# Left-side halves that land in the slots they are split into, sums built in place, and plain blocks run in pairs

## The chip, the core and the metric

The kernel runs on one core of one Trainium2 chip. The metric is the device time of one launch in microseconds (us). The kernel before took 2222.46, 2223.57 and 2224.67 us in three runs, a median of 2223.57 us. Engines are named as in the profile: PE is TensorE, DVE is VectorE, ACT is ScalarE, POOL is GpSimd, and SP is SyncE, which only issues DMAs here.

## The reference

A two-layer trunk on two request batches of 256 and 512 rows with the same weights, so 768 rows of width 2048. All data is float32.

```python
def _even_layer(x, ...):                       # layer 0
    z = _rmsnorm(x, g) @ w_in                  # q, k, v, f, ga, gf
    a = _window_attention(q, k, v, rel_bias, sink) * silu(ga)
    fo = _fourier(f, w_f, b_f) * silu(gf)
    return x + concatenate([a, fo]) @ w_out

def _odd_layer(x, ...):                        # layer 1
    z = _rmsnorm(x, g) @ w_in                  # h, bg, cg, gc, u, v, gd
    co = (bg * _short_conv(cg * h, conv_w)) * silu(gc)
    so = _spatial_gate(u, v, v_gain, w_s, b_s) * silu(gd)
    return x + concatenate([co, so]) @ w_out
```

`_rmsnorm` scales each row by the inverse root of its mean square and by a gain per column.

## The kernel before

Everything is held transposed: 128 features by 768 rows are one k-tile, and 16 k-tiles k are the left side of a product. A k-tile has two halves s of 384 rows. Each float32 product is made of three matmuls of a high and a low part (`three`: xh·wh, xl·wh, xh·wl), so every left half and every weight tile is split: ACT casts the high part (L131), and DVE subtracts it from the float32 value and writes the low part (L132; L245 and L246 where a gain is multiplied in).

Four stages follow each other: the even input projection with attention and Fourier mixing (to 801.8 us in the profile), the even output projection "stage 1" (`Out(1, ...)`), the odd input projection "stage 2" (the V columns first, 576 matmuls of 512 columns, then 24 Strassen products with the gates), and the odd output projection "stage 3" (`Out(3, ...)`). An output projection has 16 blocks of 128 output features. Blocks 0 to 3 are plain: 96 matmuls of 384 columns each. The other 12 go in 6 pairs, each by one Strassen step (`strassen`): 7 products of 8 k-tiles by 3 parts, 168 matmuls of 384 columns a pair, where two plain blocks take 192. The left quarters are A11, A12 (half 0, k-tiles 0 to 7 and 8 to 15) and A21, A22 (half 1). The products also need three sums of left quarters, S1 to S3, and S4 in place of A21; each is split into high and low.

Three times the whole left side is exchanged. At B (801.8 us) the concatenated layer-0 branches, kept in DRAM as `cat`, become the left side of stage 1. At C (1078.7 us) x1, the residual, becomes that of stage 2, and at D (1941.8 us) `cat` of layer 1 becomes that of stage 3. An exchange at B or D loads 16 k-tiles (`load_cat`, L332, at B through `row` tiles of 768 columns; at D through `ev` and `big` tiles, L902 to L905), and `build_sums` (L351) loads every k-tile again as pairs of 768-column tiles `big0` and `big1` (one of each), makes S1, S3, S2 and S4 of them (L358 to L364) in `ev` tiles, splits the sums, and writes S4 to DRAM. While the last plain block runs (`last_use`, L380), `fill` (L368) loads S4 over A21. At C the halves are loaded through `ev` tiles (L756 to L762).

PE runs its matmuls in program order. The order of ACT, DVE, POOL and SP is set by a scheduler when the kernel is built, and each engine runs its list strictly in order: what stands behind a waiting instruction waits too. SP is one list for all DMAs. There are 5 `ev` tiles of 128x384 and 5 weight tiles `wr` of 128x1024 (512 KB). The eight accumulators of PE (`bank`) hold 128x512 each; a plain block takes two, one for each half, and DVE adds the residual to a finished bank (L399), which frees it for another block. Strassen's results leave through L461 and its neighbours.

Of the kernel before, what the change touches and what calls it, by code (L numbers as in the profile page):

```python
# [17 lines left out]
P = 128  # L18
# [3 lines left out]
T = TP + TS  # L22
# [13 lines left out]
QLATE = (2, 0, 1, 3)  # L36
PW = T + 4
KV = ((8, 9, 10, 11, 12, 13, 14, 15, 0, 1, 2, 3, 4, 5, 6, 7), range(16))
# [54 lines left out]
def trunk(ctx, tc, x_t, w_in_e, w_fn, w_out_e, w_in_o, w_sv, w_out_o, w_f, w_st, b_s, sink, rel_bias,  # L93
# [143 lines left out]

    def x_slots(k, s):
        hi = xn.tile([P, H], F32R, name=f"xh{k}_{s}", tag=f"xh{k}_{s}")
        lo = xn.tile([P, H], F32R, name=f"xl{k}_{s}", tag=f"xl{k}_{s}")  # L240
        xs[k][s] = (hi, lo)
# [37 lines left out]
    class Stream:  # L279
# [13 lines left out]
        def block(self, b, tag="z", qs=range(4), flip=False, done=None):  # L293
            for q in qs:
                weights.ahead(weights.at[self.n, b, q] + RING)
                for s in ((1, 0) if flip else (0, 1)):
                    for k in range(4 * q, 4 * q + 4):
                        self.step(b, k, s, tag if tag == "z" else tag[s], k == 4 * qs[0], k == 4 * qs[-1] + 3)
                        if done:
                            done(k, s)  # L300
            return self.take(b)
# [30 lines left out]
    def load_cat():  # L332
        for k in range(KT):
            t = kept.pop(k, None)
            if t is None:
                t = row_tile()
                for s in range(2):
                    nc.sync.dma_start(out=t[:, SL[s]], in_=cat[k][:, SL[s]])
            for s in range(2):
                x_slots(k, s)  # L340
                split(*xs[k][s], t[:, SL[s]])

    late = []

    def ev():
        return late[0].tile([P, H], F32, name="ev", bufs=5)
# [4 lines left out]
    def build_sums(load, sums, order, every):  # L351

        for j in order:
            a, b = (big(i)[:, :T] for i in range(2))
            load(j, a)
            load(j + KH, b)
            s1, s3 = ev(), ev()
            nc.vector.tensor_add(out=s1, in0=a[:, SL[1]], in1=b[:, SL[1]])  # L358
            split(*sums[1][j], s1)
            nc.vector.tensor_sub(out=s3, in0=a[:, SL[0]], in1=a[:, SL[1]])  # L360
            split(*sums[3][j], s3)
            nc.vector.tensor_sub(out=s1, in0=s1, in1=a[:, SL[0]])  # L362
            split(*sums[2][j], s1)
            nc.vector.tensor_sub(out=s3, in0=b[:, SL[0]], in1=s1)  # L364
            nc.sync.dma_start(out=s4d[j], in_=s3)
            yield every

    def fill(k, h, src, t):  # L368
        nc.sync.dma_start(out=t, in_=src)
        x_slots(k, h)  # L370
        split(*xs[k][h], t)

    class Out:
# [3 lines left out]
        def __init__(self, n, pairs, qs, res, result):  # L377
            self.n, self.pairs, self.qs, self.res, self.result = n, pairs, qs, res, result

        def last_use(self, k, s):  # L380
            if s == 1 and k < KH:
                fill(k, 1, s4d[k], ev())

        def run(self):
            st = Stream(self.n)

            def load(k, t):
                nc.sync.dma_start(out=t, in_=cat[k])

            pipe.spawn(build_sums(load, sums, BUILD, BUILD_AT))  # L390
            for b in PLAIN:
                last = b == PLAIN[-1]
                if last:
                    pipe.flush()
                z = st.block(b, qs=self.qs if b == PLAIN[0] else range(4), flip=last, done=self.last_use if last else None)
                for h in range(2):
# [595 lines left out]
```

## Time and profile before

| | us |
|---|---|
| median of three runs | 2223.57 |
| the profiled execution, by the device's clock | 2220.93 |
| its span in the profile | 2219.2 |
| PE busy | 2130.9 (96%) |
| DVE busy | 1430.6 (64%) |
| ACT busy | 906.0 (41%) |
| bytes moved by DMA | 251.99 MB, mean 114 GB/s |

The span is cut below into stretches, each of which lies between two ends of a stage. A group of rows in the next section but one has a line for each stretch: the busy time of every engine in it with the number of its instructions, the TensorE clock that was granted as a share of full speed, the busy share of the DMA engines, and what they moved. A stretch in which PE is busy from end to end is bound by PE, and a stretch in which it is not is where another engine or a transfer decides. The rows of a timeline give start, duration and count of merged instructions, and in brackets the idle time just before with what ended it.

### The profile page before, as it was taken

To read this page: it belongs to the slowest core of one execution; us is meant where nothing else is said; L and a number is where in the kernel's file an instruction comes from. 1 tells how busy PE (TensorE), PEld (TensorE's weight loads), DVE (VectorE), ACT (ScalarE), POOL (GpSimd) and SP (SyncE) were. 2 spreads that over 40 slices of the span, in tenths; PEclk is the share of its full clock that TensorE was granted. 3 is DMA by queue.
4 is the path that set the end of the run, shared out by engine and by line. 5 is a ranking of instruction groups with operands and counts; after the bars stand their busy time and mean duration, and the time that the engine had idled before them with its cause. 6 is when DMAs were issued, how large, how long until landed. Compare 5 with 4: busy or idle time off the path is not lost.

```text
span 2219.2 us, 31587 instructions
## 1 busy us (share of the span) xinstructions
PE 2130.9 (96%) x12034; PEld 2082.8 (94%) x12034; DVE 1430.6 (64%) x2450; ACT 906.0 (41%) x1761; POOL 74.3 (3%) x75
## 2 busy tenths in 40 slices
PE   7999999999999986999799999999999999978999
PEld 6999999999999986999688999999999999968999
DVE  8435746737737655666676666666667777766665
ACT  6323444434534542433534333333334555533332
POOL 5000000000000000222000000000000000000000
PEclk9999999999999997999899999999999999989999
DMA  6512122121121155444568222222222322465442
GB/s 225 131 69 85 49 72 74 48 84 63 59 79 58 39 196 174 147 134 133 178 231 295 98 77 74 81 83 84 83 84 93 100 91 100 146 215 173 131 133 72
DMA packets 108737, 251.99 MB, mean 114 GB/s; under 512 B 11773, under 2 KB 56233, under 8 KB 108585
## 3 DMA queue, kind: packets, MB, share of 16 engines
q1 hardware_dynamic: 108584, 249.98, 34.2%
q8 instruction: 94, 1.54, 0.3%
q14 instruction: 59, 0.48, 0.1%
HBM read 210.58 MB, written 42.49 MB: 114 GB/s over the span
## 4 chain that ended last, share of the span: by engine, by line
PE 88%; DMA 5%; DVE 4%; ACT 2%; issue 1%; SPq 0%; DVEq 0%; ACTq 0%
PE bank L117 87%; DMA big<-cat 3%; PE bank L127 1%; DMA xr<-in_x_t_dram 1%; DVE xl L246 1%; DMA ev<-cat 1%; DMA ev<-x 0%; ACT xh L245 0%; DVE wl L132 0%; DVE xl L132 0%; DVE s1l L132 0%; ACT sc L681 0%; DVE ev L362 0%; DVE ev L358 0%; DVE s3l L132 0%
## 5 line engine op out<-in xcount | busy, mean ns | idle before, releaser
L117 PE MATMUL bank<-xh,wh 128*128 128x384 f32 x2560 | 865.5, 338 | 49.0 <-DVE ev L399 43.4
L117 PE MATMUL bank<-xl,wh 128*128 128x384 f32 x2560 | 862.6, 337 | 2.9 <-DVE xl L132 2.5
L117 PE MATMUL bank<-xh,wl 128*128 128x384 f32 x2560 | 861.3, 336 | 0.0
L131 ACT CAST wh<-wr 128x512 fp32r<-128x512 f32 x728 | 450.4, 621 | 915.6 <-PE bank L117 748.2
L132 DVE TENSOR_TENSOR wl<-wr,wh 128x512 fp32r<-128x512 f32 x728 | 503.9, 695 | 350.1 <-ACT wh L131 341.6
L117 PEld LDWEIGHTS bank<-xh,wh 128*128 128x128 f32 x2560 | 484.5, 189 | 52.5 <-DVE ev L399 44.7
L117 PEld LDWEIGHTS bank<-xl,wh 128*128 128x128 f32 x2560 | 484.8, 189 | 5.8 <-DVE xl L132 5.5
L117 PEld LDWEIGHTS bank<-xh,wl 128*128 128x128 f32 x2560 | 484.3, 189 | 0.0
L117 PE MATMUL bank<-wh,xh 128*128 128x512 f32 x288 | 116.5, 404 | 18.7 <-ACT xh L245 18.7
L117 PE MATMUL bank<-wl,xh 128*128 128x512 f32 x288 | 115.0, 399 | 0.6 <-DVE wl L132 0.6
L117 PE MATMUL bank<-wh,xl 128*128 128x512 f32 x288 | 114.8, 399 | 0.0
L117 PE MATMUL bank<-s2h,wh 128*128 128x384 f32 x288 | 97.1, 337 | 0.0
L117 PE MATMUL bank<-s1h,wh 128*128 128x384 f32 x288 | 97.0, 337 | 0.0
L117 PE MATMUL bank<-s1h,wl 128*128 128x384 f32 x288 | 96.9, 336 | 0.0
L117 PE MATMUL bank<-s3h,wl 128*128 128x384 f32 x288 | 96.8, 336 | 0.0
L117 PE MATMUL bank<-s2l,wh 128*128 128x384 f32 x288 | 96.8, 336 | 0.0
L117 PE MATMUL bank<-s2h,wl 128*128 128x384 f32 x288 | 96.8, 336 | 0.0
L117 PE MATMUL bank<-s3h,wh 128*128 128x384 f32 x288 | 96.7, 336 | 0.0
L117 PE MATMUL bank<-s1l,wh 128*128 128x384 f32 x288 | 96.6, 336 | 0.0
L117 PE MATMUL bank<-s3l,wh 128*128 128x384 f32 x288 | 96.6, 336 | 0.0
L117 PEld LDWEIGHTS bank<-wh,xh 128*128 128x128 f32 x288 | 56.0, 195 | 31.1 <-ACT xh L245 19.5
L640 DVE RECIPROCAL nrt<-nrt 128x384 f32<-128x384 f32 x32 | 81.5, 2548 | 4.8 <-ACT nrt L639 4.8
(197 smaller groups left out, 2483.1 us busy)
## 6 DMA issues: line engine op xcount, KB each, us to landing
wr<-in_w_in_o_dram SPq DMA_DIRECT2D x96, 512.0 KB, 3.3
wr<-in_w_in_e_dram SPq DMA_DIRECT2D x72, 512.0 KB, 3.3
wr<-in_w_out_e_dram SPq DMA_DIRECT2D x32, 512.0 KB, 3.4
wr<-in_w_out_o_dram SPq DMA_DIRECT2D x32, 512.0 KB, 4.0
big<-cat SPq DMA_DIRECT2D x32, 384.0 KB, 3.9
big<-x SPq DMA_DIRECT2D x28, 384.0 KB, 3.8
wr<-in_w_sv_dram SPq DMA_DIRECT2D x16, 512.0 KB, 4.0
ev<-x SPq DMA_DIRECT2D x40, 192.0 KB, 3.3
```

The costliest lines, as they stand in the source:

```text
L117: nc.tensor.matmul(out, lhsT=lhs, rhs=rhs, start=start, stop=stop, skip_group_check=go_on)
L127: nc.tensor.transpose(out=out, in_=in_, identity=ident)
L131: nc.scalar.copy(out=hi, in_=src)
L132: nc.vector.tensor_sub(out=lo, in0=src, in1=hi.bitcast(F32))
L246: nc.vector.scalar_tensor_tensor(out=lo, in0=src, scalar=g, in1=hi.bitcast(F32), op0=ALU.mult, op1=ALU.subtract)
L640: nc.vector.reciprocal(out=rt, in_=rt)
```

## The change

The left side lives in 113 slots of 128x384. Seven roles (A11, A12, A21, A22, S1, S2, S3) of eight k-tiles each have a pair of slots, one for the high and one for the low part, and one slot is spare. A half is loaded into the low slot of its pair as float32. Its high part goes to the pair's high slot, its low part to the spare slot, and the slot that held the float32 value is the new spare (`fill`). Which slots play which role is changed at every exchange (`move`): the new roles are dealt to the old slots in the order in which the last Strassen step of the stage before reads them last (`FREED`). `build_sums` loads four halves into slots of S1, S2 and S3, computes the sums in place and splits them by way of the spare slot. `big0`, `big1` are no longer its landing tiles. There are 4 `ev` tiles in place of 5, and while Strassen steps run, the spare slot serves as a further one (`extra`). The plain blocks run as two pairs: `duo` walks through the k-tiles once for two blocks and both halves, with four accumulators, and the second pair uses the other four. The order of loads at C and D is changed.

```diff
+FREED = ("A11", "S1", "S2", "A12", "S3", "A22", "A21")
...
     def out_order(src, layer, pairs):
-        first = range(4) if layer == 1 else QLATE
-        return [(src, layer, b, q) for b in PLAIN for q in (first if b == PLAIN[0] else range(4))] + [(src, layer, b, q) for b in pairs for q in range(14)]
+        plain = [(src, layer, b, q) for i in range(0, len(PLAIN), 2) for q in range(4) for b in PLAIN[i:i + 2]]
+        return plain + [(src, layer, b, q) for b in pairs for q in range(14)]
...
+    def move(*roles):
+
+        old = [[where[r, j] for j in range(KH)] for r in FREED]
+        for r, o in zip(roles, old):
+            for j in range(KH):
+                where[r, j] = o[j]
...
+        def duo(self, bs, tags, done):
+
+            for q in range(4):
+                weights.ahead(weights.at[self.n, bs[0], q] + RING)
+                for k in range(4 * q, 4 * q + 4):
+                    for s in range(2):
+                        for b, t in zip(bs, (tags[:2], tags[2:])):
+                            self.step(b, k, s, t[s], k == 0, k == KT - 1)
                         if done:
                             done(k, s)
...
     def ev():
-        return late[0].tile([P, H], F32, name="ev", bufs=5)
+        return late[0].tile([P, H], F32, name="ev", bufs=4)
+
+    def extra(dtype=F32):
+
+        return slot(spare[0], dtype) if lent[0] else ev()
...
         for j in order:
-            a, b = (big(i)[:, :T] for i in range(2))
-            load(j, a)
-            load(j + KH, b)
-            s1, s3 = ev(), ev()
-            nc.vector.tensor_add(out=s1, in0=a[:, SL[1]], in1=b[:, SL[1]])
-            split(*sums[1][j], s1)
-            nc.vector.tensor_sub(out=s3, in0=a[:, SL[0]], in1=a[:, SL[1]])
-            split(*sums[3][j], s3)
-            nc.vector.tensor_sub(out=s1, in0=s1, in1=a[:, SL[0]])
-            split(*sums[2][j], s1)
-            nc.vector.tensor_sub(out=s3, in0=b[:, SL[0]], in1=s1)
-            nc.sync.dma_start(out=s4d[j], in_=s3)
+            ids = [i for r in ("S1", "S2", "S3") for i in where[r, j]]
+            a0, a1, b1, b0 = (slot(i, F32) for i in ids[:4])
+            for k, h, t in ((j, 0, a0), (j, 1, a1), (j + KH, 1, b1), (j + KH, 0, b0)):
+                load(k, h, t)
+            if every > 5:
+                yield 3.0
+            nc.vector.tensor_add(out=b1, in0=a1, in1=b1)
+            nc.vector.tensor_sub(out=a1, in0=a0, in1=a1)
+            nc.vector.tensor_sub(out=a0, in0=b1, in1=a0)
+            nc.vector.tensor_sub(out=b0, in0=b0, in1=a0)
+            nc.sync.dma_start(out=s4d[j], in_=b0)
+            for i, src, at in ((2, a0, (ids[4], ids[5])), (3, a1, (ids[0], spare.pop())), (1, b1, (ids[1], ids[3]))):
+                where[f"S{i}", j] = list(at)
+                sums[i][j] = slots((f"S{i}", j))
+                split(*sums[i][j], src)
+            spare.append(ids[2])
             yield every
 
-    def fill(k, h, src, t):
+    def fill(k, h, src, g=None):
+        at = where[quarter(k, h)]
+        t = slot(at[1], F32)
         nc.sync.dma_start(out=t, in_=src)
+        at[1], spare[0] = spare[0], at[1]
         x_slots(k, h)
-        split(*xs[k][h], t)
+        if g is None:
+            split(*xs[k][h], t)
+        else:
+            split_gain(k, h, t, g)
...
         if b == PLAIN[0]:
             nc.scalar.activation(out=rr[:, SL[h]], in_=o, func=AF.Square)
         else:
-            sq = ev()
+            sq = extra()
             nc.scalar.activation(out=sq, in_=o, func=AF.Square)
             nc.gpsimd.tensor_add(out=rr[:, SL[h]], in0=rr[:, SL[h]], in1=sq)
...
-    Out(1, PAIRS_E, range(4), x_t, keep_sum).run()
+    Out(1, PAIRS_E, (4, 5, 6, 7), (0, 1, 2, 3), x_t, keep_sum).run()
...
-    Out(3, PAIRS_O, QLATE, x1, finish).run()
+    Out(3, PAIRS_O, (0, 1, 2, 3), (4, 5, 6, 7), x1, finish).run()
```

Three places show how the engines' lists are changed. A row is the line, the operation and its tiles, then the width, and in brackets the engines and DMA queues whose results it waits for.

First SP at B, before, around the DMAs that write the last k-tiles of `cat` (`cat9` to `cat11`) and the weights `wr`:

```order
155 L184 DMA wr_7851<-in_w_out_e_dram 128x1024 [waits DMAHW4_49,DVE_49]
156 L310 DMA cat10_7533<-at_6647 128x768 [waits DVE_49]
157 L184 DMA wr_7936<-in_w_out_e_dram 128x1024 [waits DMAHW5_49,DVE_49]
158 L338 DMA row_7538<-cat0_3081 128x384
159 L338 DMA row_7538<-cat0_3081 128x384 [waits DMAHW6_49]
160 L338 DMA row_7549<-cat1_3084 128x384 [waits DMAHW7_49,PE_49]
```

The same place of the change:

```order
153 L184 DMA wr_7497<-in_w_out_e_dram 128x1024 [waits DMAHW3_49,DVE_49]
154 L341 DMA cat9_7532<-at_6647 128x768 [waits DVE_49]
155 L409 DMA slot1_7542<-cat0_3081 128x384 [waits PE_49]
156 L409 DMA slot3_7558<-cat1_3084 128x384 [waits PE_49]
157 L409 DMA slot5_7574<-cat2_3087 128x384 [waits DMAHW4_49,PE_49]
158 L409 DMA slot7_7590<-cat3_4564 128x384 [waits DMAHW5_49,PE_49]
159 L409 DMA slot33_7550<-cat0_3081 128x384 [waits DMAHW6_49,PE_49]
```

The loads of the new left side now stand right behind `cat9`, and each waits only for PE's last read of the slot, while before they stood behind `cat10` and two weight tiles.

Second DVE at B, before, where the first plain block's results (L399) stand between the sums (L358 to L364 and the splits s1l, s2l, s3l):

```order
927 L358 TENSOR_TENSOR ev_7879<-big0_7875,big1_7876 128x384 [waits DMAHW2_49,DMAHW0_49]
928 L360 TENSOR_TENSOR ev_7880<-big0_7875 128x384
929 L132 TENSOR_TENSOR s1l6_7722<-ev_7879,s1h6_7721 128x384 [waits Activation_49]
930 L132 TENSOR_TENSOR s3l6_7754<-ev_7880,s3h6_7753 128x384 [waits Activation_49]
931 L362 TENSOR_TENSOR ev_7879<-ev_7879,big0_7875 128x384 [waits DVE_49]
932 L364 TENSOR_TENSOR ev_7880<-big1_7876,ev_7879 128x384 [waits DVE_49]
933 L399 TENSOR_TENSOR ev_7926<-bank_7780,ev_7926 128x384 [waits DMAHW6_49,DMAHW3_49]
```

The change, where the first pair's results are L446, the sums L394 to L397, and `wl_8233` is a weight tile of the second pair (blocks 2 and 3, k-tiles 4 to 7):

```order
957 L446 TENSOR_TENSOR ev_8156<-bank_7805,ev_8156 128x384 [waits PE_49]
958 L446 TENSOR_TENSOR ev_8161<-bank_7813,ev_8161 128x384 [waits DMAHW5_49,PE_49]
959 L132 TENSOR_TENSOR slot80_8122<-slot67_8105,slot66_8121 128x384 [waits Activation_49]
960 L446 TENSOR_TENSOR ev_8166<-bank_7809,ev_8166 128x384 [waits DMAHW6_49]
961 L396 TENSOR_TENSOR slot68_8180<-slot84_8182,slot68_8180 128x384 [waits DVE_49]
962 L394 TENSOR_TENSOR slot86_8207<-slot71_8206,slot86_8207 128x384 [waits DMAHW7_49,DMAHW6_49]
963 L397 TENSOR_TENSOR slot85_8183<-slot85_8183,slot68_8180 128x384 [waits DMAHW3_49,DVE_49]
964 L132 TENSOR_TENSOR slot83_8126<-slot82_8106,slot67_8125 128x384 [waits DMAHW3_49,Activation_49]
965 L132 TENSOR_TENSOR slot101_8194<-slot68_8180,slot100_8193 128x384 [waits Activation_49]
966 L395 TENSOR_TENSOR slot71_8206<-slot70_8205,slot71_8206 128x384 [waits DMAHW5_49,DVE_49]
967 L132 TENSOR_TENSOR wl_8233<-wr_7886,wh_8232 128x512
```

The results still stand between the sums, and the weight tile of the second pair stands behind 56 rows of sums, splits and results, from row 911 on.

Third DVE at C in the change, around the last result of stage 1 (L510) and the first low parts of x1 (L268, the line that was L246):

```order
1158 L510 TENSOR_TENSOR ev_10021<-bank_9954,ev_10021 128x384 [waits PE_49]
1159 L132 TENSOR_TENSOR wl_10408<-wr_10106,wh_10407 128x512 [waits Activation_49]
1160 L268 SCALAR_TENSOR_TENSOR slot15_10204<-slot112_10201,sm_83,slot0_10203 128x384 [waits DMAHW2_49,Pool_49]
1161 L268 SCALAR_TENSOR_TENSOR slot112_10210<-slot33_10207,sm_83,slot2_10209 128x384 [waits DVE_49]
1162 L132 TENSOR_TENSOR big0_10393<-rr_85,big0_10393 128x384 [waits DMAHW4_49,Activation_49]
1163 L268 SCALAR_TENSOR_TENSOR slot33_10216<-slot35_10213,sm_83,slot4_10215 128x384 [waits DMAHW5_49,DVE_49]
...
1168 L268 SCALAR_TENSOR_TENSOR slot43_10246<-slot45_10243,sm_83,slot14_10245 128x384 [waits DMAHW2_49,DVE_49]
1169 L268 SCALAR_TENSOR_TENSOR slot45_10252<-slot81_10249,sm_83,slot65_10251 128x384 [waits DMAHW3_49,DVE_49]
```

The low parts stand in one chain in which each takes the slot that the one before it has freed, and the first goes to slot 15, which POOL still reads as the square of the last result. Row 1169 is the low part of k-tile 8 in half 1.

## Rows read from the trace of the kernel before

**Rows 1.** The page: busy time of each engine, and the chain by engine

```profile
PE 2130.9 (96%) x12034; PEld 2082.8 (94%) x12034; DVE 1430.6 (64%) x2450; ACT 906.0 (41%) x1761; POOL 74.3 (3%) x75
...
PE 88%; DMA 5%; DVE 4%; ACT 2%; issue 1%; SPq 0%; DVEq 0%; ACTq 0%
```

**Rows 2.** Waits of PE: line waited for, us in total, times, longest us

```profile
PE bank L117 <- DVE ev L399: 43.4, 4, 18.1
PE bank L117 <- ACT xh L245: 18.7, 3, 9.1
```

**Rows 3.** Busy time by stretch (count), granted clock, DMA share, GB/s

```profile
802.00:870.00 68.00, 41.78 (x204) 38.99 (x204) 42.80 (x84) 28.26 (x58) 0.00 (x0) 0.81 0.59 196
...
1078.50:1100.00 21.50, 8.24 (x20) 6.03 (x20) 12.34 (x23) 12.56 (x23) 0.99 (x1) 0.68 0.74 225
1100.00:1220.00 120.00, 120.00 (x538) 99.65 (x537) 89.09 (x145) 54.53 (x103) 0.16 (x3) 1.00 0.76 258
...
1942.00:2007.00 65.00, 41.73 (x205) 38.90 (x206) 39.74 (x77) 23.62 (x48) 0.00 (x0) 0.80 0.66 212
```

**Rows 4.** The chain in order of time at B

```profile
837.66 3.97 DMA big<-cat
...
844.86 0.55 DVE ev L399
```

**Rows 5.** Timeline of DVE: the last operation of each stage

```profile
801.77 0.56 DVE L314 TENSOR_TENSOR row<-bank,rr 128x384 f32<-128x384 f32 x1 [1.53 <-PE bank L117]
...
1078.66 0.56 DVE L461 TENSOR_TENSOR ev<-bank,ev 128x384 f32<-128x384 f32 x1
...
1941.78 0.55 DVE L461 TENSOR_TENSOR ev<-bank,ev 128x384 f32<-128x384 f32 x1
...
2215.31 0.56 DVE L461 TENSOR_TENSOR ev<-bank,ev 128x384 f32<-128x384 f32 x1 [3.61 <-PE bank L117]
```

**Rows 6.** Line L461, the last result of each Strassen pair

```profile
L461 DVE TENSOR_TENSOR ev<-bank,ev x36: 514/549/558, 933.7 to 2215.3; 128x384 f32<-128x384 f32 x36
```

**Rows 7.** Busy time in two shorter stretches of B, columns as in rows 3

```profile
805.00:815.00 10.00, 8.53 (x34) 7.21 (x35) 8.44 (x18) 7.50 (x18) 0.00 (x0) 0.83 0.92 301
...
835.00:845.00 10.00, 0.00 (x0) 0.00 (x0) 5.79 (x13) 2.61 (x6) 0.00 (x0) 0.50 0.41 138
```

**Rows 8.** Timeline of SP at B: issues of left-side loads and others

```profile
778.30 0.33 SPq L310 DMA_DIRECT2D cat<-at  x1
...
804.86 10.71 SPq L338 DMA_DIRECT2D row<-cat  x18
```

**Rows 9.** Line L338, the left-side loads at B: from issue to landing

```profile
DMA to landing us min/median/max: 2.8/4.2/5.3
```

**Rows 10.** Timeline of DVE at B: low parts of left halves

```profile
804.33 2.89 DVE L132 TENSOR_TENSOR xl<-row,xh 128x384 fp32r<-128x384 f32 x6
```

**Rows 11.** Groups of DVE instructions from 802 to 870 us

```profile
L132 DVE TENSOR_TENSOR xl<-row,xh 128x384 fp32r<-128x384 f32 x26 | 12.8, 550 | 0.3 <-ACT xh L131 0.3
```

**Rows 12.** Timeline of PE at C

```profile
1082.75 0.75 PE L117 MATMUL bank<-wh,xh 128*128 128x512 f32 x1 [4.13 <-ACT xh L245]
...
1095.79 0.80 PE L117 MATMUL bank<-wh,xh 128*128 128x512 f32 x1 [9.12 <-ACT xh L245]
1096.39 0.63 PE L117 MATMUL bank<-wl,xh 128*128 128x512 f32 x1
1096.82 0.63 PE L117 MATMUL bank<-wh,xl 128*128 128x512 f32 x1
...
1100.77 0.39 PE L117 MATMUL bank<-wl,xh 128*128 128x512 f32 x1
1100.99 0.39 PE L117 MATMUL bank<-wh,xl 128*128 128x512 f32 x1
```

**Rows 13.** Timelines of POOL and DVE at C: last square added, low parts

```profile
1079.91 0.99 POOL L741 TENSOR_TENSOR rr<-rr,ev 128x384 f32<-128x384 f32 x1 [3.09 <-ACT ev L740]
...
1088.97 2.73 DVE L246 SCALAR_TENSOR_TENSOR xl<-ev,sm,xh 128x384 fp32r<-128x384 f32 x5 [1.16 <-ACT xh L245]
```

More of the change, by code (lines that the diff above doesn't have):

```diff
@@ L236, in trunk, with slot, quarter, slots @@
     xs = [[None, None] for _ in range(KT)]
-    def x_slots(k, s):
-        hi = xn.tile([P, H], F32R, name=f"xh{k}_{s}", tag=f"xh{k}_{s}")
-        lo = xn.tile([P, H], F32R, name=f"xl{k}_{s}", tag=f"xl{k}_{s}")
-        xs[k][s] = (hi, lo)
+    late = []
+    where = {}
+    for i, role in enumerate(("A11", "A12", "A21", "A22", "S1", "S2", "S3")):
+        for j in range(KH):
+            where[role, j] = [16 * i + 2 * j, 16 * i + 2 * j + 1]
+    spare = [112]
+    def slot(i, dtype=F32R):
+        pool = late[0] if 64 <= i < 112 else xn
+        return pool.tile([P, H], dtype, name=f"slot{i}")
+    def quarter(k, s):
+        return f"A{s + 1}{k // KH + 1}", k % KH
+    def slots(key):
+        return tuple(slot(i) for i in where[key])
+    def x_slots(k, s):
+        xs[k][s] = slots(quarter(k, s))
+    def move(*roles):
+        old = [[where[r, j] for j in range(KH)] for r in FREED]
+        for r, o in zip(roles, old):
+            for j in range(KH):
+                where[r, j] = o[j]
     def split_gain(k, s, src, g):
@@ L330, in trunk, with load_cat @@
     kept = {}
[L332 to L343, printed above, removed]
+    def load_cat(order):
+        for k, s in order:
+            x_slots(k, s)
+            if k in kept:
+                split(*xs[k][s], kept[k][:, SL[s]])
+            else:
+                fill(k, s, cat[k][:, SL[s]])
+        kept.clear()
+    lent = [False]
     def ev():
-        return late[0].tile([P, H], F32, name="ev", bufs=5)
+        return late[0].tile([P, H], F32, name="ev", bufs=4)
+    def extra(dtype=F32):
+        return slot(spare[0], dtype) if lent[0] else ev()
     def big(i, dtype=F32):
@@ L369, in fill, with __init__ @@
         nc.sync.dma_start(out=t, in_=src)
+        at[1], spare[0] = spare[0], at[1]
         x_slots(k, h)
-        split(*xs[k][h], t)
+        if g is None:
+            split(*xs[k][h], t)
+        else:
+            split_gain(k, h, t, g)
     class Out:
[L377 to L382, printed above, removed]
+        def __init__(self, n, pairs, first, last, res, result):
+            self.n, self.pairs, self.res, self.result = n, pairs, res, result
+            self.tags = (first, last, first)
@@ L384, in run, with load, done @@
         def run(self):
             st = Stream(self.n)
-            def load(k, t):
-                nc.sync.dma_start(out=t, in_=cat[k])
+            def load(k, h, t):
+                nc.sync.dma_start(out=t, in_=cat[k][:, SL[h]])
+            def done(k, s):
+                if s == 1 and k < KH:
+                    fill(k, 1, s4d[k])
             pipe.spawn(build_sums(load, sums, BUILD, BUILD_AT))
-            for b in PLAIN:
-                last = b == PLAIN[-1]
+            for i, tags in zip(range(0, len(PLAIN), 2), self.tags):
+                duo = PLAIN[i:i + 2]
+                last = i + 2 == len(PLAIN)
@@ L393, in run @@
                 if last:
                     pipe.flush()
-                z = st.block(b, qs=self.qs if b == PLAIN[0] else range(4), flip=last, done=self.last_use if last else None)
-                for h in range(2):
-                    res = ev()
-                    nc.sync.dma_start(out=res, in_=self.res[b][:, SL[h]])
-                    nc.vector.tensor_add(out=res, in0=z[h], in1=res)
-                    self.result(b, h, res)
+                st.duo(duo, tags, done if last else None)
@@ L401, in run @@
+                for b in duo:
+                    for h, z in enumerate(st.take(b)):
+                        res = ev()
+                        nc.sync.dma_start(out=res, in_=self.res[b][:, SL[h]])
+                        nc.vector.tensor_add(out=res, in0=z, in1=res)
+                        self.result(b, h, res)
+            lent[0] = True
             for b in self.pairs:
@@ L434, in strassen @@
             if first:
[L435 removed]
+                acc[at] = bank(tags[at], H)
             for half in range(2):
```

77 lines of the change are left out of this document (38 added, 39 removed).

## The prediction

> **What bounds the kernel now.** I read the page's busy times first: PE is busy 96% of the span, and PE holds 88% of the chain that ended last, with DMA 5% and DVE 4% behind it [rows 1]. So there is little to win except where PE waits. The view of waits says for whom: 43.4 us in four waits for the plain blocks' results on DVE (L399), and 18.7 us in three for high parts on ACT (L245) [rows 2]. A table by stretches then puts these in their places. From 1100 to 1220 us PE is busy 120.00 of 120.00 at clock 1.00. Behind each of the three exchanges it is not: 41.78 of 68 at B, 8.24 of 21.5 at C and 41.73 of 65 at D, with a granted clock of 0.81, 0.68 and 0.80 [rows 3]. These three places are the whole case.
>
> What each costs is the time of the stage less its matmuls at full clock. Line L461 stands once in each Strassen pair, from 933.7 us on [rows 6]; the six of stage 1 end at 1078.66 [rows 5], so a pair takes (1078.66 - 933.7) / 5 = 28.99 us, or 0.1726 us for each of 168 matmuls. A stage needs 6 x 28.99 + 384 x 0.1726 = 240.2 us. Stage 1 lasts 1078.66 - 801.77 = 276.9 and stage 3 2215.31 - 1941.78 = 273.5 [rows 5]: **36.7 us are lost at B and 33.3 at D.** At C the timeline has 22 matmuls before the one at 1100.77, at 0.22 us each when the clock is full [rows 12]: 1100.77 - 1078.66 - 4.8 = **17.3 us.** Together 87.3 us, the most that can be won.
>
> Why B is slow is in the chain: a pair of whole k-tiles is loaded, 3.97 us, then summed and split, then the next pair is loaded into the same two tiles, and the result of the first plain block, L399 at 844.86, stands in DVE's list behind these sums [rows 4]. In that stretch PE does nothing at all from 835 to 845, and DMA moves only 138 GB/s, against 301 at 805 to 815 [rows 7]. So it isn't the DMA's rate that limits; it is that one transfer waits for another. At C there is less to it: halves arrive in few buffers, and PE waits 4.13 and 9.12 us for high parts [rows 12].
>
> **The change, part by part.**
>
> *Loads into slots, at B.* The first load used to be issued behind the last k-tiles of the stage before, eight of them from about 795 and 18 from 804.86 at 10.71 / 18 = 0.595 us each [rows 8]. Now they stand behind `cat9`, which was issued at 778.30 [rows 8], and wait for PE's last read of the slots in the last gate block, 96 matmuls (16.6 us) before 801.77, so from 785.2 on. 26 halves fit before the stage ends, and no start wait is left. The 32 halves for the sums follow `cat11`, whose input is ready at about 804.4; from there 40 rows of SP up to the last of them take 40 x 0.595 = 24 us, to 829, or at 301 GB/s for their 8.3 MB 28 us, to 833. DVE is later than that: its first sum, row 911, needs four halves issued by about 808 and landing 4.2 us later [rows 9], 812.5.
>
> *DVE at B.* From row 911 to the second weight tile that the second pair needs for k-tiles 4 to 7 there are 64 rows. One row lasts 0.55 us [rows 11], but six in a row end 2.89 / 6 = 0.48 apart [rows 10]: 843.2 to 847.7. PE needs that tile at 801.8 + 192 x 0.1726 + 48 x 0.1726 = 843.2, with half a microsecond more for its place in the pair. So 0 to 4 us are lost; I take 2. The 43.4 us of waits for L399 go, B's and D's alike, since the second pair has four other banks and doesn't ask for the first pair's results; the next to ask is the first Strassen pair, 33 us later. Four `ev` tiles instead of five make the last results a chain of load, add and store; the sums take none of these tiles any more, so I price it at 1 us, 0 to 3. **B: 3 us left of 36.7** (0 to 7).
>
> *D.* Loads begin as the last Strassen pair frees slots, from 1941.78 - 28.99 = 1912.8. The first sum in DVE's list waits for the 34th half; with four weight tiles and a `cat` tile 9.2 MB stand up to there, 30.6 us at 301 GB/s, so 1943.4, and the in-order list behind it stands still until then. 18 rows later comes a weight tile of the first pair that PE wants at 1941.8 + 8.3 + 0.5 = 1950.6: 1943.4 + 18 x 0.48 (0.55) = 1952 to 1953.3. 87 rows on, the second pair's tile, wanted at 1983.2, is there at 1985 to 1991. The larger holds, since a loss at the first moves the second's due time: 2 to 8. **D: 6 us left of 33.3** (2 to 10), on the later side, as `cat15` is written only after the stage's last result and SP's list stands behind it.
>
> *C.* High parts and loads are now there when the stage ends, as their slots come free inside the last Strassen pair. But the first low part goes to the spare slot, which `keep_sum` has lent out for the last square: POOL reads it until 1079.91 + 0.99 = 1080.9 [rows 13]. This is a new wait, and behind it on DVE stand all low parts, each taking the slot that the one before frees. PE does two matmuls (they need high parts alone) and then waits. From 1081.5 it has k-tile 8 of half 0, nine matmuls at 0.43 us at the half clock [rows 12], to 1085.4. Then it needs half 1, the ninth low part: 1081.5 + 8 x 2.73 / 5 [rows 13] + 0.5 for one split between = 1086.4. The loss is 1086.4 - 1078.66 - 11 x 0.22 = 5.3, and up to 2.7 more until the clock is back (before, 13 matmuls from 1095.79 took 4.98 us where 2.9 would do). **C: 7 us left of 17.3** (5.3 to 8).
>
> *At nothing:* the move of roles and of banks, the same number of Strassen matmuls, and half-width `xhat` operations, which lie beside the V stage where PE is busy 120 of 120; without that cover 16 more of them at 0.55 cost 9 us.
>
> *A rule that speaks against the pairs.* V's matmuls already go round six banks, three matmuls to each, in the stretch of clock 1.00 and full PE [rows 3]. The Trainium skill, "TensorE: Matmul & The Clock Gate", section "A second HAM failure mode: psum-queue depth-cycling", says that cycling through the accumulator banks every iteration leaves the engine idle so often that its clock swings between its two levels. The pairs go round four banks in the same manner. The trace disagrees: clock 1.00 through these 120 us. What it would give here is the last rival.
>
> Sum: 87.3 - 3 - 6 - 7 = 71.3 us won. The profiled execution took 2220.93 us for a span of 2219.2 (between them 1.7 us of start and end, untouched): 2149.6. The median of the runs is 2.6 us above the profiled one: **2152 us**. With all low ends (0, 2, 5.3) 2143.5, with all high ones (7, 10, 8) 2161.
>
> **The rivals.**
>
> 1. DVE's list becomes the bound. For it: DVE has to make all sums in order with weights and results among them. In the stretch at B it did 84 instructions in 68 us, 0.81 each with its waits, at D 77 in 65, 0.84 [rows 3]. At that pace B's 64 rows take 52 us, 21 late, and D's 87 take 73, 33 late; with 8 for C, 62 us stay lost: 2198. Against: most of those waits were for loads into two tiles, which go. Midway, near 2178, is more like it than the end.
>
> 2. The loads don't come earlier. Slots might come free only with the stage's end. Then only the 43.4 us for L399 are won [rows 2]: 2180. Against: each load waits for PE alone, and the first roles read are the first refilled.
>
> 3. Nothing is late but C's spare slot: DVE at 0.48 and no more stalls, 2144 or less.
>
> 4. Slower: the exchange is bound by transfers, each half waiting for another, at the 138 GB/s of 835 to 845 us [rows 7]. SP issues 15.3 MB from 785.2 to the last half of B and 17.5 MB from 1912.8 at D: 111 and 127 us, due at 843.2 and 1983.2, so 53 and 56 lost, plus 7: 28.7 more than now, 2252. It decides below (15.3 + 17.5) / (58 + 70 + 80) = 158 GB/s, the 80 being 87.3 less C's 7. Against: 18 halves were issued in 10.71 us, 330 GB/s [rows 8].
>
> 5. The pairs' round of four banks halves the granted clock: their 768 matmuls would cost another 768 x 0.1726 = 133 us, and 2152 + 133 gives 2285. Against: V's round of six at 1.00 [rows 3].
>
> **How the numbers follow.** The forecast, 2143 to 2161, gets 0.45; rival 1 0.28; rival 2 0.08; rival 3 0.11; rival 4 0.04; rival 5 0.01; something else that leaves the time within 0.2%, about what a measurement of this kernel can tell from no change, 0.03. The range goes from 2142, near the sum with all low ends, to 2184, which takes in rival 2 and the half of rival 1 below its end. Faster 0.92, within 0.2% 0.03, slower 0.05.
>
> **What would show it.** The waits of PE for the plain blocks' results gone from their 43.4 us; PE busy without a gap from 802 to about 835; a short PE wait near 843 into stage 1 and near 1950 for a weight's low part; at C two matmuls, then a wait for a low part of about 3 us and another of about 1. Wrong would be: PE waiting for a left half's load at B, a DMA rate under 200 GB/s in the first 40 us of B or D, or a granted clock under 0.9 where PE has no gap.

## The result, and the profile after

The changed kernel took 2163.03 us (median of 4 runs, 2160.78 to 2164.63) against 2223.50 us before: a ratio of 0.9727, with a 95% interval of 0.971 to 0.9744. The forecast was 2152 us, in a range of 2142 to 2184. The direction and the places were right; the gain was 60.5 us instead of 71, and the time lies 2 us above the band from 2143 to 2161 to which the prediction gave 0.45.

The page of the changed kernel, busy times and the chain by engine, which answer to [rows 1]:

```profile
span 2160.4 us, 31653 instructions
PE 2120.9 (98%) x12034; PEld 2074.6 (96%) x12034; DVE 1429.5 (66%) x2466; ACT 898.9 (42%) x1761; POOL 75.0 (3%) x75
PE 90%; DVE 3%; DMA 3%; ACT 2%; issue 1%; SPq 0%; DVEq 0%; ACTq 0%
```

What PE waits for in the changed kernel (line, us in total, times, longest), which answers to [rows 2]:

```profile
PE bank L117 <- DVE wl L132: 9.4, 5, 3.1
PE bank L561 <- DVE cwl L564: 6.7, 1, 6.7
PE bank L127 <- DVE sc L736: 6.0, 4, 1.5
PE bank L117 <- DVE slot L268: 5.9, 3, 3.8
PE bank L117 <- ACT slot L267: 5.4, 1, 5.4
PE bank L117 <- DVE ev L504: 1.2, 1, 1.2
```

The 43.4 us for plain blocks' results are gone, as is most of the 18.7 us for high parts (the 5.4 left are at the kernel's start). L561 and L127 are in layer 0 and the change doesn't touch them. New are waits for low parts: of weights (`wl`), and of x1 at C (L268).

The stretches behind the three exchanges, changed kernel; columns as in [rows 3]:

```profile
802.00:842.00 40.00, 40.00 (x233) 40.00 (x232) 36.66 (x73) 18.96 (x39) 0.00 (x0) 1.00 0.88 287
842.00:862.00 20.00, 14.33 (x70) 13.69 (x69) 14.22 (x27) 10.40 (x22) 4.03 (x2) 0.83 0.83 268
1052.00:1070.00 18.00, 12.40 (x41) 9.47 (x41) 14.65 (x25) 6.77 (x11) 1.46 (x2) 0.81 0.90 297
1900.00:1960.00 60.00, 56.20 (x320) 55.20 (x319) 54.75 (x111) 27.13 (x56) 0.00 (x0) 1.00 0.85 285
```

Where B left PE idle from 835 to 845 us before, it now runs 40 us without a gap, at clock 1.00, while DMA moves 287 GB/s. Then it stumbles: of the next 20 us it is busy for 14.33. At D there are small gaps only.

For the account by stage I take the starts of PE's matmuls. A stage ends where the next one's first matmul starts, or where the stage's last one would have made room for it. These are the borders of the changed kernel:

```profile
802.43 0.33 PE L117 MATMUL bank<-slot,wl 128*128 128x384 f32 x1
802.60 0.51 PE L117 MATMUL bank<-slot,wh 128*128 128x384 f32 x2
...
1052.70 0.39 PE L117 MATMUL bank<-wh,slot 128*128 128x512 f32 x1
...
1197.02 0.34 PE L117 MATMUL bank<-slot,wh 128*128 128x384 f32 x1
...
1911.56 0.33 PE L117 MATMUL bank<-slot,wh 128*128 128x384 f32 x1
...
2156.50 0.33 PE L117 MATMUL bank<-slot,wl 128*128 128x384 f32 x1
```

| stretch, us | before | after | difference |
|---|---|---|---|
| to the end of layer 0's blocks | 801.6 | 802.6 | +1.0 |
| stage 1 (B at its start) | 276.9 | 250.1 | -26.8 |
| V (C at its start) | 150.0 | 144.3 | -5.7 |
| rest of stage 2 | 711.4 | 714.5 | +3.1 |
| stage 3 (D at its start) | 275.3 | 245.1 | -30.2 |

Undisturbed matmuls of 384 columns start 0.17357 us apart on the mean in stage 1, so a stage of 1392 takes 241.6 us, not the 240.2 of the prediction (which divided times of L461, where DVE adds its own delays). By this B lost 35.3 us before and loses 8.5 now; D lost 33.7 and loses 3.5, with 1.2 more inside the last Strassen pair of stage 2.

### The profile page after: what moved, and what is told of

The parts are those of the page before. It is cut to its first block, busy times and chain, and to the rows that moved or that the text cites. A ratio compares the mean times of both kernels' runs of the same rounds, so it can differ in the third digit from the quotient of the medians.

```text
span 2160.4 us, 31653 instructions
## 1 busy us (share of the span) xinstructions
PE 2120.9 (98%) x12034; PEld 2074.6 (96%) x12034; DVE 1429.5 (66%) x2466; ACT 898.9 (42%) x1761; POOL 75.0 (3%) x75
## 3 DMA queue, kind: packets, MB, share of 16 engines
q1 hardware_dynamic: 116360, 248.01, 35.3%
## 4 chain that ended last, share of the span: by engine, by line
PE 90%; DVE 3%; DMA 3%; ACT 2%; issue 1%; SPq 0%; DVEq 0%; ACTq 0%
PE bank L117 89%; DMA slot<-cat 1%; PE bank L127 1%; DMA xr<-in_x_t_dram 1%; DMA s<-slot 1%; DVE slot L268 1%; DVE slot L132 1%; DVE wl L132 0%; ACT sc L730 0%; DVE slot L395 0%; DVE slot L397 0%; ACT L730 0%; ACT L350 0%; DVE slot L396 0%; DVE slot L394 0%
## 5 line engine op out<-in xcount | busy, mean ns | idle before, releaser
L117 PE MATMUL bank<-slot,wh 128*128 128x384 f32 x6848 | 1747.0, 336 | 1.3 <-DVE ev L504 1.2
L117 PEld LDWEIGHTS bank<-slot,wh 128*128 128x128 f32 x6848 | 1236.1, 188 | 2.1 <-issue 1.5
L117 PE MATMUL bank<-slot,wl 128*128 128x384 f32 x3424 | 1150.0, 336 | 8.3 <-DVE wl L132 8.3
L117 PEld LDWEIGHTS bank<-slot,wl 128*128 128x128 f32 x3424 | 643.4, 188 | 9.6 <-DVE wl L132 9.6
L117 PE MATMUL bank<-wh,slot 128*128 128x512 f32 x576 | 187.1, 403 | 11.3 <-DVE slot L268 5.9
L117 PEld LDWEIGHTS bank<-wh,slot 128*128 128x128 f32 x576 | 111.0, 193 | 37.8 <-DVE slot L268 7.6
L131 ACT CAST slot<-slot 128x384 fp32r<-128x384 f32 x176 | 87.2, 512 | 108.0 <-DVE slot L132 37.4
L132 DVE TENSOR_TENSOR slot<-slot,slot 128x384 fp32r<-128x384 f32 x176 | 97.3, 557 | 31.9 <-ACT slot L131 24.3
L117 PE MATMUL bank<-wl,slot 128*128 128x512 f32 x288 | 115.3, 401 | 1.1 <-DVE wl L132 1.1
L345 DVE TENSOR_TENSOR row<-bank,rr 128x384 f32<-128x384 f32 x40 | 22.3, 557 | 39.6 <-PE bank L117 39.6
L200 DVE TENSOR_TENSOR wr<-wr 128x1024 f32<-128x1024 f32 x36 | 47.6, 1322 | 1.2
L202 DVE TENSOR_TENSOR wr<-wr 128x1024 f32<-128x1024 f32 x36 | 44.1, 1226 | 1.2
L196 DVE TENSOR_TENSOR wr<-wr 128x1024 f32<-128x1024 f32 x36 | 44.0, 1221 | 0.5
L198 DVE TENSOR_TENSOR wr<-wr 128x1024 f32<-128x1024 f32 x36 | 43.9, 1220 | 0.4
L790 POOL TENSOR_TENSOR rr<-rr,slot 128x384 f32<-128x384 f32 x24 | 35.3, 1473 | 130.2 <-ACT slot L789 130.2
L268 DVE SCALAR_TENSOR_TENSOR slot<-xr,sm,slot 128x384 fp32r<-128x384 f32 x32 | 36.5, 1184 | 3.2 <-ACT slot L267 3.2
```

Source lines behind the costliest of these rows:

```text
L117: nc.tensor.matmul(out, lhsT=lhs, rhs=rhs, start=start, stop=stop, skip_group_check=go_on)
L131: nc.scalar.copy(out=hi, in_=src)
L132: nc.vector.tensor_sub(out=lo, in0=src, in1=hi.bitcast(F32))
L196: nc.vector.tensor_sub(out=w11, in0=w12, in1=w11)
L198: nc.vector.tensor_sub(out=w11, in0=w22, in1=w11)
L200: nc.vector.tensor_sub(out=w12, in0=w22, in1=w12)
```

## The experiments

Every run's time is compared with the changed kernel's 2163.03 us, and its ratio is to runs of the kernel before on the same chip. The runs were spread over three chips, on which the kernel before took 2222.99 to 2224.41 us in the median. Stretches of a stage are read from the traces, one execution of each kernel. An edit that is shown in part is marked by three dots.

**1. The pairs without the slots.** The kernel before with `duo` and eight banks:

```diff
...
-                z = st.block(b, qs=self.qs if b == PLAIN[0] else range(4), flip=last, done=self.last_use if last else None)
...
+                st.duo(PLAIN[i:i + 2], tags, range(4) if last else self.qs, self.last_use if last else None)
...
```

> The kernel before with its plain blocks run in pairs on eight banks, and nothing else of the change. Theory (the early loads are the gain): the waits of PE for the plain blocks' results, 43.4 us, go, but the sums are still made from two landing tiles one after another, ready only near 869 us and 2006 us, so PE waits for them instead: 2212 to 2224 us. Rival (the banks held back by results that stand behind the sums are the loss): about 43 us less, 2180 us.

Measured: 2207.42 us, 0.993 of before (0.9915 to 0.9945). Nearer to the theory than to the rival, though 5 us below its range. In the stretch at B the waiting has moved 33 us on:

```profile
802.00:870.00 68.00, 65.45 (x369) 64.88 (x368) 44.23 (x83) 30.54 (x61) 0.00 (x0) 0.97 0.72 235
870.00:920.00 50.00, 22.75 (x104) 21.23 (x103) 29.32 (x49) 16.07 (x32) 6.63 (x6) 0.71 0.53 163
```

PE gets through the plain blocks, 65.45 us of 68, and then stands for 27 of 50. PE's waits from 870 to 920 us, and a row of DVE's timeline:

```profile
PE bank L117 <- ACT ev L459: 16.1, 1, 16.1
PE bank L117 <- ACT s1h L131: 10.6, 2, 8.3
PE bank L117 <- DVE s1l L132: 0.6, 1, 0.6
```

```profile
908.96 0.56 DVE L412 TENSOR_TENSOR ev<-bank,ev 128x384 f32<-128x384 f32 x1 [3.20 <-DMA ev<-in_x_t_dram]
```

Only 11.2 us of it are for sums, which are still made one pair of tiles after another. The 16.1 us are for ACT's copy of the first Strassen product (L459). It stands in ACT's list behind the squares of the second pair's four results, and three of these results (L412) wait some 3 us each for the load of their residual, one after the other. So at B nothing is won (stage 1 takes 279.1 us in this trace, 276.9 before); what is won lies at D (stage 3 takes 262.5 instead of 275.3). The 43.4 us in [rows 2] could not be had by more banks alone: take the wait away and the next ones take its place, and one of those comes from the pairs themselves.

**2. The slots without the pairs.** The changed kernel, blocks one at a time, each on two banks of its own:

```diff
...
-            for q in range(4):
-                weights.ahead(weights.at[self.n, bs[0], q] + RING)
-                for k in range(4 * q, 4 * q + 4):
-                    for s in range(2):
-                        for b, t in zip(bs, (tags[:2], tags[2:])):
+            for b, t in zip(bs, (tags[:2], tags[2:])):
+                for q in range(4):
+                    weights.ahead(weights.at[self.n, b, q] + RING)
+                    for k in range(4 * q, 4 * q + 4):
+                        for s in range(2):
...
```

> The changed kernel with its plain blocks one after another, each on two banks of its own, and S4 loaded during the last block alone. Theory (the early loads into freed slots are the gain, and the pairs add little as long as every block has its own banks): 2160 to 2175 us. Rival (the pairs are needed, since they ask for the left side and for the first weights half as fast and give the loads of S4 33 us instead of 17): PE waits for low parts or for S4, 2185 us or more.

Measured: 2152.86 us, 10 us less than the change. Better than both expectations: from 800 to 1040 us PE waits for nothing at all, and stage 1 takes 241.5 us, its matmuls and no more. The pairs not only add nothing to the slots, they cost 10 us.

**3. Roles dealt the other way.**

```diff
-FREED = ("A11", "S1", "S2", "A12", "S3", "A22", "A21")
+FREED = ("A21", "A22", "S3", "A12", "S2", "S1", "A11")
```

> The changed kernel, where at the exchanges C and D the new roles are dealt to the old slots in the reverse order, so that the quarters loaded first get the slots that the last Strassen pair frees last. B is as in the change. Theory (loads inside the last Strassen pair are what is won at C and D): C loses about 8 us more than now and D 15 to 27 us: 2186 to 2198 us. Rival (DVE's list is the bound whenever the loads come): 2160 to 2168 us.

Measured: 2169.25 us, 6 us more than the change, and between the two expectations. Most of what it costs lies at D, where PE now waits for the first halves, in this trace from 1890 to 1930 us:

```profile
PE bank L117 <- DVE slot L132: 4.5, 1, 4.5
PE bank L117 <- ACT slot L131: 3.1, 1, 3.1
```

The order of dealing is worth 6 us, not 23, and that is a sum: in this trace stage 3 takes 9.1 us more than in the change and V 1.7 more, while the rest of stage 2 takes 3.0 less. There the quarters lie in other slots, which run 9 shows to matter, and the wait of 1.2 us in the last pair is gone. Seven products free their slots over 29 us, and even dealt badly 35 of the 62 loads from `cat` at D are issued before stage 2 ends, 41 in the change.

**4. A shorter lead for the weights.** As 2, with tiles split one later:

```diff
...
-                    weights.ahead(weights.at[self.n, b, q] + RING)
+                    weights.ahead(weights.at[self.n, b, q] + RING - 1)
...
```

> The changed kernel with its plain blocks one after another (as in slots_alone, 2152.86 us), and their weight tiles split one tile later: three tiles ahead of use instead of four, so that a tile has 8.3 us instead of 12.4 us in DVE's list before PE wants it, as the two tiles of a pair have. Theory (what the pairs lose at B is the short lead of their weight tiles in DVE's in-order list): PE waits for low parts of weights at B, 4 to 8 us more: 2156 to 2161 us. Rival (the loss comes from the pairs' results or loads, not from the lead): 2151 to 2155 us.

Measured: 2150.05 us (2147.95 to 2152.5), 1 us below the rival's range, and no wait at B. My theory falls: a short lead alone does no harm.

**5. S4 out of the way.** Now for DVE's list itself. In the changed kernel, rows of DVE's timeline at B (the first is the first sum; `s<-slot` is the write of S4), with what ended the idle time, and PE's two waits:

```profile
815.95 0.56 DVE L394 TENSOR_TENSOR slot<-slot,slot 128x384 f32<-128x384 f32 x1 [1.09 <-DMA slot<-cat]
...
831.25 0.56 DVE L132 TENSOR_TENSOR slot<-slot,slot 128x384 fp32r<-128x384 f32 x1 [1.10 <-DMA s<-slot]
...
845.62 1.03 DVE L132 TENSOR_TENSOR slot<-slot,slot 128x384 fp32r<-128x384 f32 x2 [1.48 <-DMA s<-slot]
847.03 0.69 DVE L132 TENSOR_TENSOR wl<-wr,wh 128x512 fp32r<-128x512 f32 x1
```

```profile
847.77 0.44 PE L117 MATMUL bank<-slot,wl 128*128 128x384 f32 x1 [3.06 <-DVE wl L132]
...
851.18 0.69 PE L117 MATMUL bank<-slot,wl 128*128 128x384 f32 x1 [2.62 <-DVE wl L132]
```

The split of S1 writes its low part over the slot from which S4 is just being written to DRAM, so it waits until that transfer has landed, and the weight tile that PE wants stands just behind it. The experiment computes S4 into a landing tile that lies idle:

```diff
-            nc.vector.tensor_sub(out=b0, in0=b0, in1=a0)
-            nc.sync.dma_start(out=s4d[j], in_=b0)
+            s4 = big(j % 2)[:, :H]
+            nc.vector.tensor_sub(out=s4, in0=b0, in1=a0)
+            nc.sync.dma_start(out=s4d[j], in_=s4)
```

> The changed kernel, where S4 is computed into a landing tile of its own instead of in place, so that S1's low part needn't wait until the DMA that writes S4 has landed. Theory (these waits, 2.7 us at B and 1.7 us at D in DVE's list, come out at PE's waits for weights): B loses 3 to 4 us less and D 1 us less, 2157 to 2160 us. Rival (DVE has slack for them elsewhere, or S4's own tiles bring the wait back): 2161 to 2164 us.

Measured: 2159.47 us, in the theory's range, but for a sum of two things. PE's wait at B falls from 5.7 us to one line of this trace:

```profile
PE bank L117 <- DVE wl L132: 1.0, 2, 0.8
```

Yet from the first Strassen pair on, the matmuls are slower on the mean: 0.1746 us apart in stage 1 instead of 0.1736, 0.1749 in stage 2 instead of 0.1740. Over 1008 + 4032 + 1008 matmuls of the pairs that is some 5.5 us given back. It isn't every matmul: of the 1008 in stage 1's pairs 89 take about 0.181 us, against 12 in the change, and most of the others are as before.

**6. The same, with the slots' addresses mended.** A landing tile takes up 3104 bytes a partition. In run 5 the two are allotted earlier, among the slots, and move those behind them: six of the 113 slots now start 32 bytes off a multiple of 64, and others are moved by whole multiples.

```diff
-        return late[0].tile([P, PW], dtype, name=f"big{i}")
+        return late[0].tile([P, 800], dtype, name=f"big{i}")[:, :PW]
```

> As s4_aside, with each of the two landing tiles 3200 bytes a partition instead of 3104, so that the slots laid out behind them start on multiples of 64 bytes again (in s4_aside some start 32 bytes off). Theory (the slower matmuls of s4_aside, 0.1746 us apart instead of 0.1736 in stage 1, come from the slots' addresses): 0.1736 again in stage 1 and 0.174 in stage 2, some 5 us less than s4_aside: 2152 to 2156 us. Rival (they come from the extra tiles' traffic or the chip's state): 0.1746 again, 2158 to 2161 us.

Measured: 2152.81 us, 10 us less than the change, with matmuls of stage 1 0.1736 us apart again. So with S4 aside the pairs win back most of what they lost at B (stage 1 takes 243.4 us instead of 250.1), and the slots' addresses hid it in run 5. With it gone the pairs are level with the blocks one at a time (2152.86). Two things stay open. The edit also changes the order of DVE's list: between the two weight tiles that PE waits for stand two rows instead of six, and no run separates this from the waits for S4. And it isn't shown that the 32 bytes slow the matmuls, as the padding moves other slots too: in run 5 77 of the 89 slow matmuls, and the one behind each of them, read slots that start on multiples of 64.

**7. The last square out of the spare slot.** This is the wait that the prediction named at C.

```diff
-            sq = extra()
+            last = (b, h) == (PAIRS_E[-1][1], 0)
+            sq = stage1.r[1][:, SL[0]] if last else extra()
...
```

> The changed kernel, where the square of stage 1's very last result goes to a residual tile that is no longer needed, so that the spare slot is free for the first low part at C. Theory (POOL's read of the square in the spare slot holds back the chain of low parts): PE's first wait at C falls from 3.8 us to under 2 us, the second one too, 2158 to 2161 us. Rival (DVE's list itself, with the last results and weights ahead of the low parts, is as late): 2162 to 2164 us, the wait stays at 3 us or more.

Measured: 2163.02 us (2157.52 to 2166.82), no difference. The four runs lie too far apart to settle a gain of 2 us, but the traces do: V with its wait lasts 144.1 us, 144.3 in the change. The changed kernel has the two waits that were foretold, behind POOL's read of the square:

```profile
1055.42 0.99 POOL L790 TENSOR_TENSOR rr<-rr,slot 128x384 f32<-128x384 f32 x1 [2.95 <-ACT slot L789]
```

```profile
1057.12 1.22 PE L117 MATMUL bank<-wh,slot 128*128 128x512 f32 x2 [3.79 <-DVE slot L268]
...
1062.69 0.73 PE L117 MATMUL bank<-wh,slot 128*128 128x512 f32 x2 [1.81 <-DVE slot L268]
```

With the square elsewhere the first is gone and the second takes its whole time:

```profile
1053.15 0.39 PE L117 MATMUL bank<-wl,slot 128*128 128x512 f32 x1
1059.40 1.22 PE L117 MATMUL bank<-wh,slot 128*128 128x512 f32 x2 [5.86 <-DVE slot L268]
```

PE waits for k-tile 8 of half 1, the ninth low part. The chain and the loads set its time, and the square only decided where in front of it PE stood.

**8. C by k-tile.** As 2, with the square aside, and the halves of a k-tile next to each other:

```diff
...
-    old = [(k, h) for ks in (range(KH, KT), range(KH)) for h in range(2) for k in ks if k not in newest]
+    old = [(k, h) for ks in (range(KH, KT), range(KH)) for k in ks for h in range(2) if k not in newest]
```

> The kernel of slots_alone (2152.86 us), with the last square out of the spare slot, and at C both halves of a k-tile loaded and split next to each other, not eight first halves ahead of eight second ones. Theory (PE waits at C for the second half of its first k-tile, the ninth low part of a chain): V with its wait lasts 138 to 141 us instead of 144.5, 2147 to 2150 us. Rival (the loads decide at C, which share the DMA engines with weights at 331 GB/s): 143 to 145 us, 2151 to 2154 us.

Measured: 2142.65 us (2141.6 to 2143.75), 10 us below slots_alone and 4 us below the theory's range. V with its wait lasts 136.6 us instead of 144.5, and one PE wait of 0.62 us is left of C:

```profile
1045.65 0.73 PE L117 MATMUL bank<-wh,slot 128*128 128x512 f32 x2 [0.62 <-DVE slot L268]
```

Two things differ from run 2 here, the square and the order. Run 7 shows that the square alone wins nothing; the order alone was not run, so whether it needs the square out of its way stays open.

**9. Quarters kept in the first pool.** V's matmuls were slower in the change, with PE busy all the time. In the changed kernel and, below it, in the one before, PE's matmuls (count behind its busy time) in 100 us of V:

```profile
1080.00:1180.00 100.00, 100.00 (x435) 81.25 (x434) 74.82 (x141) 40.21 (x76) 0.00 (x0) 1.00 0.57 189
```

```profile
1120.00:1220.00 100.00, 100.00 (x443) 82.81 (x442) 71.32 (x121) 41.74 (x81) 0.16 (x3) 1.00 0.78 268
```

435 against 443; on the mean of V they start 0.2312 us apart, against 0.2267. In the change slots 0 to 63 and the spare lie in one pool (a piece of the on-chip memory that is allotted at once), 64 to 111 in a second one; after an exchange of roles a quarter can lie in either. In the change's V A11 and A22 lie in the second pool, and by the order of the matmuls those that read them start 0.2333 and 0.2335 us apart, those of A12 and A21, in the first, 0.2284 and 0.2295. The experiment:

```diff
-    move("A12", "A22", "A11", "A21", "S1", "S2", "S3")
+    move("A12", "S1", "S2", "A22", "S3", "A11", "A21")
```

> The changed kernel with other roles at C: the four left quarters stay in the slots of the first pool and the sums in the second pool's, as they lie in stage 1. Theory (a stationary operand in the second pool's slots makes V's matmuls slower, 0.2331 against 0.2284 us where all is in the first): V's matmuls start 0.2267 to 0.228 us apart again, 1.7 to 2.5 us won in V and up to 1.7 in the Strassen pairs of stage 2, less up to 2 us at C, as the second quarter's slots come free later: 2159 to 2162 us. Rival (the spacing has to do with the banks or with what DVE and DMA do in this stretch): spacing stays at 0.231, 2163 to 2165 us.

Measured: 2160.11 us (2159.01 to 2161.43), and in the same 100 us of V:

```profile
1080.00:1180.00 100.00, 100.00 (x443) 82.73 (x442) 75.92 (x145) 39.62 (x76) 0.00 (x0) 1.00 0.56 189
```

443 again. The Strassen pairs of stage 2 are back at 0.1736 us, from 0.1740. Run 3 lies between, as only A11 was in the second pool there: 0.2332 us in that quarter, 0.2294 on the mean. It is the slots' place, then, and neither the banks nor the traffic; what about the address decides it (all slots start at multiples of 64 bytes here) wasn't tried.

**10 and 11. All of it together.**

> c_by_tile with S4 in landing tiles of 3200 bytes, and the roles at C as in roles_kept. Theory: V's matmuls 0.2267 to 0.228 us apart (2 us), the Strassen pairs of stage 2 at 0.1736 (1.8 us), D up to 1 us: 2142 to 2146 us. Rival (the second quarter's slots come free too late for the order by tile): what is won in the spacing is lost in waits at C, 2147 to 2150 us.

> all_mended with the roles at C dealt as in the change. Theory: as c_by_tile, less up to 1 us at D: 2146 to 2149 us, 3 to 4 us above all_mended. Rival: equal to all_mended or below it, since the second quarter's slots come free earlier.

Measured: 2141.17 us (2140.83 to 2142.62) with the quarters kept, which is 0.9628 of before (0.9612 to 0.9644) and 22 us below the change, and 2143.16 us (2142.42 to 2144.66) with roles dealt as in the change. Both lie below their ranges. On the same chip c_by_tile took 2142.65, so with the blocks one at a time S4 in landing tiles brings nothing that can be seen. The difference between the two is 2 us, not 4. The matmuls gave the 4 us, but PE's waits at C in the run with the quarters kept took 2 back:

```profile
PE bank L117 <- DVE big L132: 1.6, 1, 1.6
PE bank L117 <- DVE ev L505: 0.8, 1, 0.8
PE bank L117 <- DVE slot L268: 0.3, 1, 0.3
```

The first is for a low part of the norm's sum, the second for a result of the last Strassen pair, and neither stands in the other run. The wait for the left side's own low parts is 0.3 us, 0.6 in the other run, so the slots that come free later are not what PE waits for; why DVE is later with these two wasn't tried. With the quarters kept PE is busy 99% of the span:

```profile
PE 2111.5 (99%) x12034; PEld 2069.7 (97%) x12034; DVE 1427.2 (67%) x2466; ACT 900.9 (42%) x1761; POOL 76.0 (4%) x75
```

## Why the prediction was right, and where it was 11 us short

*What bounds it.* Right: the three exchanges were the whole case, and PE's own work the floor. Of 86 us lost there (87.3 by the prediction's sum, with its matmul 0.6% too short) some 64 came back, and 5 were lost elsewhere. None of the three signs of being wrong came: PE waits for no load at B, DMA moves 287 GB/s in the first 40 us of B and 285 from 1900 to 1960 us at D, and the granted clock is 1.00 in the 40 us in which PE has no gap.

*Loads into slots, at B.* Right in the mechanism: no start wait, and 287 GB/s from 802 to 842 us, where the prediction asked for more than 200. One step of it was late. The splits of halves loaded early stand in DVE's list ahead of layer 0's last results, which came at 802.81 and 804.68 us. In DVE's timeline:

```profile
804.22 0.55 DVE L132 TENSOR_TENSOR slot<-slot,slot 128x384 fp32r<-128x384 f32 x1
804.68 0.55 DVE L345 TENSOR_TENSOR row<-bank,rr 128x384 f32<-128x384 f32 x1
...
806.55 0.95 DVE L354 TENSOR_TENSOR at<-row,at 128x768 f32<-128x768 f32 x1
```

L345 was L314 of [rows 5], at 801.77 there. `cat11` is written behind L354, and the loads for the sums stand behind that on SP. The first sum began at 815.95 us, not 812.5.

*DVE at B: the step that failed.* "So 0 to 4 us are lost; I take 2." From 815.95 us on, the 64 rows took until 851.1 us, 0.55 apart, the upper of the two paces given; and the 3.4 us of late start came on top. The pace holds 2.7 us of waits for S4's landing, which runs 5 and 6 took away: the prediction counted the write of S4 as a row of SP and not as a wait of the split that comes after it. Without these waits the rows would be 0.51 apart, so the late start weighs no less than they do. PE lost 5.7 us in two waits, and some 2 us more while the granted clock was at 0.50, the lower of its two levels (1.2 GHz), behind them:

```profile
849.00:852.00 3.00, 0.82 (x3) 0.82 (x4) 2.88 (x6) 2.87 (x7) 2.70 (x1) 0.50 1.03 363
```

B kept 8.5 us, not 3. The chain of load, add and store of the last results, priced at 1 us, cost PE 0.2.

*The pairs.* The prediction credited the 43.4 us to the banks. Runs 1 and 2 say otherwise: the pairs alone won 15.6 us, by their trace all of it at D, and cost 10 where the slots were there already. Moving S4 brought most of these back (run 6). In run 2 DVE's list has waits for S4's landing too, 1.6 us at B, and they reach PE nowhere. My reading, which no run separates, is that the pairs' results, four at once, and their weights, two at once, stand so close in DVE's list that one stall of it reaches PE. That their weights' lead is short was my first theory, and run 4 shows that the lead by itself does no harm.

*D.* The estimate of 6 us was close: 3.5 in stage 3 and 1.2 in the pair before it.

*C.* Its two waits came where they were foretold, 3.8 and 1.8 us long instead of about 3 and 1. With the matmuls at the lower clock around them V's start kept 9.2 us (144.3 less 576 x 0.2312 and 1.95 us for the 16 matmuls of the norm), more than the 7 foretold and than the 8 at the end of its range. By the same account C had lost 17.4 us before, as the prediction had it. Its "up to 2.7 more until the clock is back" doesn't follow from the numbers beside it, 4.98 and 2.9, which give 2.1. And the cause named for the first wait was not enough: run 7 took it away and won nothing, and run 8, which also turned the order of the halves, won nearly all.

*At nothing.* Here 4.2 us were missed: V's matmuls 2.5 us slower in sum, and the Strassen pairs of stage 2 1.7 us, since the roles had moved into other slots. The move of roles was priced at nothing with no row to show it.

*The rivals.* The first, DVE's list as the bound, is what happened at B, at a smaller price: 8.5 us stay lost there, where the prediction took 3 and this rival 21. The transfers did not limit, and the pairs' banks did not slow the clock: 1.00 from 802 to 842 us with 233 matmuls recorded. The 1.0 us at the end of layer 0 is scatter: in the profiles of the eleven experiments this end lies from 0.5 us before to 1.7 us behind that of the kernel before, in run 1 with the very same code there.

## What to carry to other kernels

A wait that a profile puts on top is worth only the distance to the next one behind it: 43.4 us of bank waits were worth 15.6 until the sums came earlier, and nothing after. When a buffer is written in place and then sent out, ask who writes there next, and what stands behind that instruction in its engine's list. Load and split in the order in which the consumer asks, element by element, before looking for a faster way to do either.

## What the runs showed of the hardware

The place of PE's operands changes its rate, with no wait to be seen. With two of the four left quarters in the second pool, 512-column matmuls started 0.2312 us apart on the mean instead of 0.2267, with one there 0.2294 (runs 3 and 9; the runs 2, 4 and 7, with the roles dealt as in the change, show 0.2311 or 0.2312). With the slots moved by two landing tiles between them, 384-column ones started 0.1746 us apart instead of 0.1736, and tiles 96 bytes longer brought the 0.1736 back (runs 5 and 6). What about the address decides it is not shown. Over the 6048 matmuls of the pairs it is worth some 5.5 us, more than many an edit of the order brings.
